# First unit's adaLN sums in two groups of two, with a new table of issue, in a two-layer trunk on one core

## The chip, the cores and the metric

One core of a Trainium2 chip runs the whole kernel. The metric is the device time of one execution in microseconds. The kernel before was timed three times: 294.76 us is the median (294.72 to 295.25).

## What is computed

The reference is a decoder trunk of two layers on one sequence of 256 tokens with 1024 features, all in float32. Each layer takes its shift, scale and gate from a conditioning vector `c` (adaLN), normalises, mixes and adds:

```python
for layer in range(DEPTH):                                   # DEPTH = 2
    ada = jnp.einsum('bd,de->be', c_act, w_ada[layer]) + b_ada[layer]
    shift, scale, gate = jnp.split(ada, 3, axis=-1)          # 1024 each
    h = rms_norm(x, norm_g[layer]) * (1.0 + scale[:, None, :]) + shift[:, None, :]
    y = even_mixer(h, ...) if layer % 2 == 0 else odd_mixer(h, ...)
    x = x + gate[:, None, :] * y
return rms_norm(x, final_g)
```

The even mixer projects `h` once (w_in_even), runs two groups of attention heads on the result, multiplies by gate paths and projects out. The odd mixer does the same with one group of 16 heads. The change concerns the product `c_act` times the shift and scale columns of `w_ada[0]`, which must be known before the first projection can use `h`.

## The kernel before, in words

The five engines are the tensor engine (PE), the vector engine (DVE), the scalar engine (ACT), GpSimd (POOL) and SyncE (SP); most transfers are started from SP's queue, and a few, `crow` (the vector c) and the first rows of biases among them, from ACT's. The projections run as three matmuls in a reduced float32 form, on a high and a low part of each operand (`whi`, `wlo`, `hhi`, `hlo`, made by ACT's casts and DVE's subtractions). The small sums of adaLN and the transposes run in full float32.

**The order of the work.** The program is first recorded: each call on an engine goes through `Plan.record`, gets the next number and a list of the records that it depends on. Then `Plan.issue` goes through the table `ORDER` of 3002 numbers and issues the records in that order. Each engine works strictly through its own part of that list, so the table decides what stands ahead of what on every engine and queue. `plan.group` ties records together only in their dependencies: every member of a group then waits for what any member waits for. As nearly all instructions are issued by one line of `Plan.issue`, the profile gives L244 for nearly all; tiles are what tells them apart.

**The start.** The input `x` comes into `xs`. ACT and DVE normalise it into the tiles `t` (one per half of the tokens), PE transposes these by a product with `ta` (an identity) in 16 pieces of 128x128 into the banks `ps_s` and `ps_pj`, and DVE and ACT copy them to `bigA`. PE also transposes `crow`; from it ACT and DVE make `cz`, where the activated c stands in column 0 of 32 with zeros beside it. Between these stand 26 dummy matmuls (`WARM`, `ps_o<-ones`), whose result is never used.

**The units.** The first projection consumes `h` in units of 2, 2, 2 and 2 tiles of 128 features (`START`). For each unit the loop at the end of the start loads the shift and scale columns of `w_ada[0]` and the rows of the projection's weights, calls `start_sums` to get this unit's shift and scale, `start_prep` to make `hhi` and `hlo`, and `start_mm` for the matmuls into the seven accumulating banks. `start_sums` has n = 2 tiles and d of the eight terms of each sum made by DVE beforehand (d = 0, 4, 4, 6). It has four sums to make, q = 0 and 1 the shift of the two tiles, q = 2 and 3 their scale. Each is a chain of matmuls with `cz[:, k]` as the stationary operand, 32 output rows and 128 columns, at rows 32q of one bank (`tile_position=(0, 32q)`), so that four of them with different q can use four quarters of the array. They are recorded with k outside and q inside, and tied together in fours. The first unit (d = 0) thus has 32 such matmuls: the tile `qT0` holds the shift columns for k = 0 to 3, `qT1` those for k = 4 to 7, `qT2` the scale columns for k = 0 to 3, and `gate` (in two loads) those for k = 4 to 7. Behind the sums, ACT copies the bank to `asb`, PE transposes it (`ps_m<-ta,asb`), DVE adds the bias and multiplies by the norm's weight, and `start_prep` can run. The second unit's weights are in `late`, the third's in `qT` and `gate` again, the fourth's in `late` again; in those units a DVE sum `acc` stands as one more term.

**The end.** The last projection ends in pieces. For the last 256 columns of the second half of the tokens, DVE adds PE's last bank to `xs` and forms the last sum of squares (`ISA parts`, in the profile CUSTOM_DVE_ANT_0 and its accumulator's read), POOL takes the root, and the output block is scaled (384 and 256 columns) and stored by SP and ACT. The 640 columns of the first half's output block, `t41` from `xs` and `parts`, are scaled by one instruction of DVE and stored by SP.

Of the kernel before, what the change touches and what calls it, by code (L numbers as in the profile page):

```python
# [255 lines left out]
def tile_trunk(  # L256
# [23 lines left out]
    plan = Plan(tc.nc)  # L280
# [433 lines left out]
    def start_sums(g, n, d, w):  # L714
# [29 lines left out]
        for o in range(0, len(ids), 4):  # L744
            plan.group(ids[o : o + 4])
# [640 lines left out]
```

## Time and profile before

| what | value |
|---|---|
| three runs | 294.76 us median, 294.72 to 295.25 |
| the profiled execution's own time | 295.04 us |
| its span, first to last instruction | 293.3 us |
| mean granted clock of PE | 0.995 |
| PE busy | 285.4 us (97%), 2293 instructions |
| DVE busy | 252.8 us (86%) |
| ACT busy | 188.5 us (64%) |
| DMA | 71.72 MB, mean 245 GB/s |
| chain that ended last | PE 82%, DMA 11% |

The profiled execution lies 0.28 us above the median, and 1.7 us of it lie outside the span. Times in the rows are microseconds from the start of the span; durations of single matmuls overlap, since they are pipelined, so the time that one takes is read from its start to the next one's start. A full-float32 matmul passes twice and leaves two records; in a row that joins several, the count is of records.

### The profile page before, as it was taken

What the parts mean: (1) busy time and instruction counts of PE and PEld (TensorE: products, weight loads), DVE (VectorE), ACT (ScalarE), POOL (GpSimd) and SP (SyncE); (2) the same over time, 40 slices, a digit from 0 to 9 for tenths busy, and PEclk for the clock granted to TensorE, in tenths of its full rate; (3) what the DMA queues carried; (4) which work ended last, traced back from release to release, by engine and by line L of the source; (5) the groups of instructions that cost most, each with busy time, mean ns of one, the idle gap of its engine ahead of it and who ended that gap; (6) DMA issues with size and microseconds to landing.
All of it is one profiled execution on the core that took longest, in us unless ns stands there. A gap on an engine that the chain in (4) does not pass through costs nothing.

```text
span 293.3 us, 6197 instructions
## 1 busy us (share of the span) xinstructions
PE 285.4 (97%) x2293; PEld 246.6 (84%) x2293; DVE 252.8 (86%) x629; ACT 188.5 (64%) x480; POOL 8.1 (3%) x33
## 2 busy tenths in 40 slices
PE   8999999999999999999999999999999999999991
PEld 8888788897897888777767899998899999887891
DVE  0497797999999999999889759779978999899884
ACT  4456256895998899994457863366658368584531
POOL 3000000000000000000020000000000000000021
PEclk9999999999999999999999999999999999999998
DMA  7999999999969942769986954569489709502003
GB/s 262 381 365 380 384 380 349 344 349 322 389 233 359 351 147 74 249 234 332 333 256 206 349 167 135 191 242 283 146 258 291 244 0 335 205 36 72 1 3 142
DMA packets 48431, 71.72 MB, mean 245 GB/s; under 512 B 2490, under 2 KB 33938, under 8 KB 48402
## 3 DMA queue, kind: packets, MB, share of 16 engines
q1 hardware_dynamic: 47906, 70.93, 70.6%
q8 instruction: 18, 0.29, 0.4%
q10 hardware_dynamic: 496, 0.41, 0.4%
q14 instruction: 11, 0.09, 0.1%
HBM read 70.28 MB, written 1.05 MB: 243 GB/s over the span
## 4 chain that ended last, share of the span: by engine, by line
PE 82%; DMA 11%; DVE 1%; ACT 1%; issue 1%; POOL 1%; POOLq 0%; DVEq 0%; ACTq 0%
PE ps_pj L244 53%; PE ps_s L244 10%; PE ps_o L244 7%; PE ps_pt L244 7%; PE ps_m L244 5%; DMA gate<-in_w_ada_dram 3%; DMA late<-in_w_ada_dram 3%; DMA raw<-in_w_in_even_dram 3%; DMA qT<-in_w_ada_dram 2%; DMA xs<-in_x_dram 1%; DVE wlo L244 1%; ACT t L244 1%; ACT whi L244 1%; POOL parts L244 1%; DVE t L244 0%
## 5 line engine op out<-in xcount | busy, mean ns | idle before, releaser
L244 ACT CAST whi<-raw 128x512 fp32r<-128x512 f32 (+2 forms) x116 | 71.8, 658 | 27.1 <-PE ps_pj L244 16.5
L244 DVE TENSOR_TENSOR wlo<-raw,whi 128x512 fp32r<-128x512 f32 (+2 forms) x100 | 71.3, 740 | 7.3 <-ACT whi L244 6.6
L244 PE MATMUL ps_pj<-hlo,whi 128*128 128x256 f32 x256 | 70.0, 288 | 0.0
L244 PE MATMUL ps_pj<-hhi,whi 128*128 128x256 f32 x256 | 69.9, 289 | 0.0
L244 PE MATMUL ps_pj<-hhi,wlo 128*128 128x256 f32 x256 | 68.3, 284 | 0.0
L244 PEld LDWEIGHTS ps_pj<-hhi,whi 128*128 128x128 f32 x256 | 46.7, 188 | 1.6 <-issue 0.7
L244 PEld LDWEIGHTS ps_pj<-hlo,whi 128*128 128x128 f32 x256 | 47.1, 189 | 0.8 <-issue 0.7
L244 PEld LDWEIGHTS ps_pj<-hhi,wlo 128*128 128x128 f32 x256 | 46.7, 189 | 0.3
L244 ACT ACTIVATE late<-late,mn 128x128 f32<-128x128 f32 (+1 forms) x58 | 26.0, 450 | 9.2 <-DVE mn L244 9.1
L244 DVE SCALAR_TENSOR_TENSOR acc<-raw,cz,acc 128x1024 f32<-128x1024 f32 x24 | 30.6, 1276 | 0.1
L244 PE MATMUL ps_pj<-whi,hlo 128*128 128x512 f32 (+2 forms) x72 | 25.6, 373 | 0.0
L244 PE MATMUL ps_pj<-wlo,hhi 128*128 128x512 f32 (+2 forms) x72 | 25.5, 372 | 0.0
L244 DVE SCALAR_TENSOR_TENSOR wlo<-raw,whi 128x512 fp32r<-128x512 f32 x32 | 21.1, 686 | 4.5 <-ACT whi L244 4.4
L244 PE MATMUL ps_pj<-whi,hhi 128*128 128x512 f32 (+2 forms) x72 | 24.8, 373 | 0.0
L244 PE MATMUL ps_pj<-wlo,ghi 128*128 128x512 f32 (+1 forms) x56 | 20.6, 371 | 0.0
L244 PE MATMUL ps_pj<-whi,ghi 128*128 128x512 f32 (+1 forms) x56 | 20.6, 371 | 0.0
L244 PE MATMUL ps_pj<-whi,glo 128*128 128x512 f32 (+1 forms) x56 | 20.4, 367 | 0.0
L244 PE MATMUL ps_pt<-ta,late 128*128 128x128 f32 x87 | 19.6, 275 | 0.0
L244 ACT COPY late<-ps_pt 128x384 f32<-128x384 f32 (+1 forms) x29 | 14.0, 483 | 7.9 <-PE ps_pt L244 7.6
L244 PEld LDWEIGHTS ps_pj<-whi,hhi 128*128 128x128 f32 x72 | 13.4, 188 | 2.5 <-ACT hhi L244 0.7
L244 PEld LDWEIGHTS ps_pj<-whi,hlo 128*128 128x128 f32 x72 | 13.6, 188 | 2.0 <-issue 0.2
L244 PEld LDWEIGHTS ps_pj<-wlo,hhi 128*128 128x128 f32 x72 | 13.4, 189 | 1.6
(243 smaller groups left out, 591.0 us busy)
## 6 DMA issues: line engine op xcount, KB each, us to landing
raw<-in_w_in_odd_dram SPq DMA_DIRECT2D x16, 1024.0 KB, 5.7
raw<-in_w_ada_dram SPq DMA_DIRECT2D x8, 1024.0 KB, 8.3
raw<-in_w_ada_dram SPq DMA_DIRECT2D x16, 512.0 KB, 6.3
raw<-in_w_in_even_dram SPq DMA_DIRECT2D x5, 1024.0 KB, 7.9
raw<-in_w_in_even_dram SPq DMA_DIRECT2D x7, 652.0 KB, 7.6
late<-in_w_ada_dram SPq DMA_DIRECT2D x16, 256.0 KB, 6.8
raw<-in_w_out_even_dram SPq DMA_DIRECT2D x4, 1024.0 KB, 5.8
raw<-in_w_out_odd_dram SPq DMA_DIRECT2D x4, 1024.0 KB, 8.7
```

The lines of the kernel that those rows point to most:

```text
L244: self.ops.append(dict(key=eng.key, deps=deps, fn=lambda: getattr(real, name)(*args, **kw)))
```

## The change

The records of `start_sums` are made in another order where d is 0, which is the first unit alone: first all eight steps of the two shift sums, then all eight of the two scale sums, tied together in twos. The other units keep the fours. The computed values are the same sums in the same order of k. The table `ORDER` is new from its first line on; two of its lines are shown, one taken out and one put in its place.

```diff
-5 0 45 4 9 685 2 3 6 10 37 7 1 85 11 40 38 35 86 12 87 13 14 15 16 17 70 18 88 19 89 20 71 21 72 22 55 23 46 41 39 42 47
+5 0 37 4 45 9 6 41 8 3 10 2 7 43 35 39 42 88 11 1 87 12 85 13 14 15 16 70 17 18 86 71 89 48 72 19 90 49 55 20 685 50 73
...
         ids = []
-        for m in range(max(len(tq) for tq in terms)):
-            for q, tq in enumerate(terms):
-                if m < len(tq):
+        size = 4 if d else 2
+        for o in range(0, 4, size):
+            for m in range(max(len(tq) for tq in terms)):
+                for q in range(o, o + size):
+                    tq = terms[q]
+                    if m >= len(tq):
+                        continue
                     ids.append(T.matmul(
                         pa[32 * q : 32 * q + 32, :P],
...
                         tile_position=(0, 32 * q),
                     ))
-        for o in range(0, len(ids), 4):
-            plan.group(ids[o : o + 4])
+        for o in range(0, len(ids), size):
+            plan.group(ids[o : o + size])
```

What the new table does is seen in the engines' lists. The first place is PE's list around the first unit's sums. Numbers behind an underscore are those of buffers, `x2` is a count of equal instructions in a row, and L244 of before is L245 of the change, whose table is one line longer. Before, the sums stand in one piece, shift and scale by turns:

```order
L244 MATMUL ps_s1_93<-ta_63,t41_89 128x128 x3
L244 MATMUL ps_m0_107<-qT0_98,cz_72 32x128 x2
L244 MATMUL ps_m0_107<-qT2_100,cz_72 32x128 x2
...
L244 MATMUL ps_m0_107<-qT1_99,cz_72 32x128 x2
L244 MATMUL ps_m0_107<-gate_77,cz_72 32x128 x2
L244 MATMUL ps_s1_93<-ta_63,t41_89 128x128
L244 MATMUL ps_pj1_95<-ta_63,t43_91 128x128
L244 MATMUL ps_m0_107<-ta_63,asb0_108 128x128
L244 MATMUL ps_pj1_95<-ta_63,t43_91 128x128
L244 MATMUL ps_o0_68<-ones_67 128x128
L244 MATMUL ps_pj1_95<-ta_63,t43_91 128x128
L244 MATMUL ps_o0_68<-ones_67 128x128 x3
L244 MATMUL ps_s1_93<-whi0_110,hhi_82 128x512
```

In the change the same place of PE's list reads:

```order
L245 MATMUL ps_m0_107<-qT2_100,cz_72 32x128 x8
L245 MATMUL ps_m0_107<-gate_77,cz_72 32x128 x2
L245 MATMUL ps_m0_107<-qT0_98,cz_72 32x128 x8
L245 MATMUL ps_m0_107<-gate_77,cz_72 32x128 x2
L245 MATMUL ps_s0_92<-ta_63,t41_89 128x128 x2
L245 MATMUL ps_m0_107<-qT1_99,cz_72 32x128 x8
L245 MATMUL ps_m0_107<-gate_77,cz_72 32x128 x4
L245 MATMUL ps_o0_68<-ones_67 128x128 x2
L245 MATMUL ps_m0_107<-ta_63,asb0_108 128x128
L245 MATMUL ps_o0_68<-ones_67 128x128 x5
L245 MATMUL ps_s0_92<-whi0_110,hhi_82 128x512
```

The sums now go by tiles: four pairs of scale, one more, four pairs of shift, one of scale, two transposes, then the rest of both. Four transposes of `t`, which stood behind the sums, have moved ahead of or between them, and seven dummies stand behind them where four stood. Ahead of the sums, PE has 22 dummies and 12 transposes of `t` before (15 dummies ahead of the transpose of `crow`), and 19 dummies and 14 transposes in the change (10 dummies ahead of that transpose).

The second place is the second unit's sums on PE, with the weights in `late`. Before they stand in one piece among the first unit's projection:

```order
L244 MATMUL ps_pj1_95<-wlo2_116,hhi_82 128x512
L244 MATMUL ps_s1_93<-whi2_112,hlo_83 128x512
L244 MATMUL ps_m0_107<-late_81,cz_72 32x128 x12
L244 MATMUL ps_m0_107<-acc0_106,ones_67 32x128 x4
L244 MATMUL ps_m0_107<-late_81,cz_72 32x128 x4
L244 MATMUL ps_pt0_85<-wlo3_117,hhi_82 128x256
```

In the change the first four of them come early in PE's list, six projection matmuls behind the first one:

```order
L245 MATMUL ps_pj1_95<-whi0_110,hhi_82 128x512
L245 MATMUL ps_pj2_96<-whi0_110,hhi_82 128x512
L245 MATMUL ps_m0_107<-late_81,cz_72 32x128 x4
L245 MATMUL ps_pt0_85<-whi1_111,hhi_82 128x256 x2
L245 MATMUL ps_pj2_96<-wlo0_114,hhi_82 128x512
```

The other sixteen follow some thirty rows later in one piece. On SP's queue, the loads of the first unit's adaLN weights go `gate`, `qT2`, `qT0`, `qT1`, `gate` where they went `qT0`, `qT1`, `qT2`, `gate`, `gate`, and the small loads of biases for later stages (`rows`, `srow`) come earlier. On ACT's queue the first rows of biases are started behind the table load, and no longer ahead of it.

The third place is the end of DVE's list. Before, the scaling of the 640 columns stands ahead of the last additions:

```order
L244 TENSOR_TENSOR xs_61<-xs_61,bigA_84 128x512
L244 TENSOR_SCALAR t41_89<-xs_61,parts_75 128x640
L244 TENSOR_TENSOR xs_61<-xs_61,bigA_84 128x256
L244 TENSOR_TENSOR xs_61<-xs_61,bigA_84 128x512
L244 TENSOR_TENSOR xs_61<-xs_61,ps_pj1_95 128x256
L244 ISA t42_90,parts_75<-xs_61,parts_75 128x256
L244 ISA parts_75 128x1
L244 TENSOR_SCALAR t40_88<-xs_61,parts_75 128x384
L244 SCALAR_TENSOR_TENSOR t40_88<-xs_61,parts_75,bigA_84 128x256
```

In the change it stands behind the last sum of squares:

```order
L245 TENSOR_TENSOR xs_61<-xs_61,bigA_84 128x512
L245 TENSOR_TENSOR xs_61<-xs_61,bigA_84 128x256
L245 TENSOR_TENSOR xs_61<-xs_61,ps_pj1_95 128x256
L245 ISA t42_90,parts_75<-xs_61,parts_75 128x256
L245 ISA parts_75 128x1
L245 TENSOR_SCALAR t41_89<-xs_61,parts_75 128x640
L245 TENSOR_SCALAR t40_88<-xs_61,parts_75 128x384
L245 SCALAR_TENSOR_TENSOR t40_88<-xs_61,parts_75,bigA_84 128x256
```

The scaling has moved past five instructions, the last addition of PE's result among them. PE's last 70 rows are the same in both.

231 rows, old and new, of the table ORDER are left out of this document.

## The prediction

> **What bounds the kernel now.** I read the busy time by stage first, then the chain of work that ended last, then the timeline of the tensor engine (PE) at the places that the change moves. By stage (columns: stretch and its length, then busy time of each engine with its number of instructions, granted clock, DMA share, GB/s):
>
> ```profile
> core 0: us, PE busy (x) PEld busy (x) DVE busy (x) ACT busy (x) POOL busy (x), PEclk, DMA share, GB/s
> 7.00:14.70 7.70, 7.66 (x110) 6.67 (x108) 3.65 (x13) 3.09 (x8) 0.71 (x3) 1.00 1.08 384
> 14.70:32.00 17.30, 17.30 (x125) 14.68 (x124) 14.91 (x31) 9.28 (x21) 0.00 (x0) 1.00 1.07 372
> 32.00:45.00 13.00, 12.50 (x118) 10.27 (x118) 11.08 (x23) 5.45 (x12) 0.00 (x0) 1.00 1.06 384
> 45.00:274.00 229.00, 229.00 (x1841) 197.69 (x1842) 210.08 (x535) 160.96 (x421) 2.48 (x7) 1.00 0.70 238
> ```
>
> PE fills every stretch except for 0.5 us between 32 and 45. Its last matmul starts at 286.78:
>
> ```profile
> 286.78 0.27 PE L244 MATMUL ps_pj<-whi,glo 128*128 128x256 f32 x1
> ```
>
> So from 7 to 287 us the program lasts as long as PE's list of work. The chain puts DMA ahead of PE only near the start; its row for the second half of the tile `gate`, the last adaLN weight of the first unit, gives issue and time to landing:
>
> ```profile
> 4.16 7.62 DMA gate<-in_w_ada_dram
> ```
>
> It has landed at 4.16 + 7.62 = 11.78. PE's timeline up to the first projection (start, duration, operation, out<-in, records; a full-float32 matmul leaves two records, a transpose one):
>
> ```profile
> 7.67 1.38 PE L244 MATMUL ps_o<-ones 128*128 128x128 f32 x10
> 8.88 0.27 PE L244 MATMUL ps_pj<-ta,t 128*128 128x128 f32 x1
> 8.99 0.39 PE L244 MATMUL ps_o<-ones 128*128 128x128 f32 x2
> ...
> 11.05 1.18 PE L244 MATMUL ps_m<-qT,cz 128*32 128x128 f32 x34
> ...
> 12.06 0.28 PE L244 MATMUL ps_m<-qT,cz 128*32 128x128 f32 x2
> 12.07 0.28 PE L244 MATMUL ps_m<-gate,cz 128*32 128x128 f32 x2
> ...
> 12.73 0.28 PE L244 MATMUL ps_m<-gate,cz 128*32 128x128 f32 x2
> 12.94 0.33 PE L244 MATMUL ps_s<-ta,t 128*128 128x128 f32 x1
> 13.10 0.27 PE L244 MATMUL ps_pj<-ta,t 128*128 128x128 f32 x1
> ...
> 14.74 0.70 PE L244 MATMUL ps_s<-whi,hhi 128*128 128x512 f32 x2
> ```
>
> The first sums run from 11.05 to 12.94, and the landing at 11.78 was past when PE came to the last fours. So PE's own list, and not the landing, decides that the first projection starts at 14.74. What the change adds to that list ends up in the time, unless it falls into the one wait at 32.
>
> **The sums in pairs.** The 32 matmuls of the first unit stay. A matmul with 32 output rows takes a quarter of the array, and four of them with different quarters run together. The third unit's sums give the price of a four, and hold the wait:
>
> ```profile
> 31.82 0.58 PE L244 MATMUL ps_pj<-whi,hhi 128*128 128x408 f32 x2
> 32.89 0.64 PE L244 MATMUL ps_m<-qT,cz 128*32 128x128 f32 x16 [0.50 <-DMA qT<-in_w_ada_dram]
> ...
> 33.57 0.40 PE L244 MATMUL ps_m<-acc,ones 128*32 128x128 f32 x8
> 33.79 0.40 PE L244 MATMUL ps_m<-gate,cz 128*32 128x128 f32 x8
> ```
>
> From 33.57 to 33.79 one four (8 records) takes 0.22 us, and eight fours 8 x 0.22 = 1.76. No pair of 32-row matmuls stands in this trace. The nearest rows are the pairs of 64-row matmuls of the attention values:
>
> ```profile
> 91.20 1.52 PE L244 MATMUL ps_o<-late,vb 128*64 128x256 f32 x16
> 92.65 0.49 PE L244 MATMUL ps_s<-late,qT 64*128 64x128 f32 x4
> ```
>
> These 16 records are four pairs, two of 256 and two of 128 columns; 2 x 0.44 + 2 x 0.22 = 1.32, and 1.45 was taken with the change of shape behind them. So a pair costs what a four costs. The first unit then has 16 steps in the place of 8, or +1.76, if no pair overlaps another. But at three seams of the new order a scale pair stands next to a shift pair, which write other quarters, and the rows at 12.06 and 12.07 show matmuls from two buffers begin 0.01 apart when their quarters differ. Then it is 13 steps, +5 x 0.22 = +1.10. I take 1.10, for that row shows the mechanism, and keep 1.76 as the upper end. The Trainium skill, TensorEngine Tiling (Array Packing), section Key Properties, says that different tiles can load weights and multiply in parallel. By that rule the sum is the 1.10 too, by a strict reading of the groups 1.76; the fours of this trace agree with the rule, and no run here has a seam.
>
> **Changes of shape.** The new order puts two transposes between the first unit's sums, and sends the second unit's first four ahead alone. Each is one more trip of PE into 32-row shape and back. Its price, from the second unit's sums:
>
> ```profile
> 21.51 0.39 PE L244 MATMUL ps_pj<-wlo,hhi 128*128 128x512 f32 x1
> 21.74 0.40 PE L244 MATMUL ps_s<-whi,hlo 128*128 128x512 f32 x1
> 22.07 0.86 PE L244 MATMUL ps_m<-late,cz 128*32 128x128 f32 x24
> ...
> 23.08 0.43 PE L244 MATMUL ps_m<-late,cz 128*32 128x128 f32 x8
> 23.43 0.39 PE L244 MATMUL ps_pt<-wlo,hhi 128*128 128x256 f32 x1
> 23.66 0.35 PE L244 MATMUL ps_o<-whi,hlo 128*128 128x408 f32 x1
> ```
>
> The 512-column matmul at 21.74 takes 0.33 to its successor where the one at 21.51 took 0.23 (+0.10); the last four 0.35 where 0.22 is usual (+0.13); the 256-column one at 23.43 takes 0.23, twice its usual half of a 512 (+0.11). That is 0.34 a trip. Around transposes it is 0.21 - 0.11 = 0.10 in front of 12.94 and 0.16 - 0.11 = 0.05 behind it, and with 0.10 going in again about 0.27.
>
> **The start, added up.** Of 26 dummies, 4 stood behind the sums, of 16 transposes of x 4 (the `asb` one apart); now 7 and none, with two transposes among the sums. So ahead of the sums stand 3 dummies fewer (2 records of 0.11 each) and 2 transposes more (0.11, from 8.88 to 8.99): -0.66 + 0.22 = -0.44. Then +1.10, two transposes +0.22 and their trip +0.27: the sums end 1.15 later. From the last sum to the first projection it was 14.74 - 12.73 = 2.0, a chain of copy, transpose, scale and shift on three engines, which stays; the seven dummies in it (7 x 0.22 = 1.54) fit. I take off 0.1 for the first transposes: at 7.67 ten dummy records last to 8.88, 1.21 where 1.11 would do, since PE waited there for the scalar engine's half, which the new order has earlier. So the first projection at 14.74 + 1.05 = 15.8. The vector and scalar engines lose nothing: weights and their casts get a microsecond more of lead.
>
> From there on: +0.34 for the second unit's trip. Against it stands the wait: from 31.82 two 408-column matmuls take 0.37 and the change of shape 0.10, so PE was ready at 32.29 and began at 32.89. At 1.4 us later it is ready at 33.7, behind that landing, and 0.60 of the delay is gone; what is late next is the fourth unit's landing, below. PE's balance is +1.05 + 0.34 - 0.60 = +0.8.
>
> **The rest of the order.** From 45 to 274 the same matmuls of the same shapes stand in another order, and PE was full there (229.00 of 229.00). There is nothing to win but short waits inside that busy span, and nothing to lose but new ones: 0, with 0.3 either way as my choice. SP's small loads that move ahead (16 rows of 512 bytes) weigh nothing at 372 GB/s.
>
> **The end.** PE's last 70 rows are the same. Behind them the vector engine (DVE) changes:
>
> ```profile
> 285.84 0.55 DVE L244 TENSOR_SCALAR t<-xs,parts 128x640 f32<-128x640 f32 x1
> ...
> 287.25 0.41 DVE L244 TENSOR_TENSOR xs<-xs,ps_pj 128x256 f32<-128x256 f32 x1
> ...
> 288.22 0.08 DVE L244 DVE_READ_ACCUMULATOR2_ANT parts<- 128x1 f32 x1
> 288.96 0.42 DVE L244 TENSOR_SCALAR t<-xs,parts 128x384 f32<-128x384 f32 x1 [0.67 <-POOL parts L244]
> ```
>
> PE is done at 286.78 + 0.27 = 287.05, but DVE came only at 287.25, held by its queue. Now the scaling of the 640 columns (0.55) stands behind the last sum of squares, in the wait of 0.67 for POOL's root, and no longer ahead of it: DVE is free in time, -0.15. But that block's 320 KB go out later:
>
> ```profile
> 286.43 3.81 SPq L244 DMA_DIRECT2D out_dram<-t  x3
> 287.10:288.20 1.10, 0.00 (x0) 0.00 (x0) 0.95 (x3) 0.00 (x0) 0.00 (x0) 1.00 0.74 298
> 290.10:292.00 1.90, 0.00 (x0) 0.00 (x0) 0.00 (x0) 0.00 (x0) 0.00 (x0) 0.59 0.78 276
> ```
>
> They went in 1.1 us, some 0.7 after their issue at 286.43; the last four pieces (1.90 us at 276 GB/s) followed from 290.1. Now the block is issued near 288.7, moves from 289.4 to 290.5, and the last pieces, 0.15 earlier at 290.0, share half a microsecond with it: 0.5 - 0.15 = +0.35 at most, -0.15 if the sharing is free. I take +0.2.
>
> **The sum** against the profiled execution: 295.04 + 0.8 + 0.2 = 296.0. That run is 0.28 above the median of 294.76, so the median to expect is 294.76 + 1.0 = 295.8. A measurement here tells about 0.2%, 0.59 us, from no change.
>
> **Rivals.** *The front moves up by half a microsecond more (no change).* The transpose of `crow` now stands behind 10 dummies, not 15, and what waits for it can start up to two microseconds sooner. DVE was held by it:
>
> ```profile
> 7.98 0.16 DVE L244 SCALAR_TENSOR_TENSOR tiny<-tiny,ps_pt 128x8 f32<-128x8 f32 x1 [1.24 <-ACT tiny L244]
> ```
>
> If more of PE's time ahead of 11.05 was hand-over than the 0.1 that I see, the first projection comes at 15.3, and with the end at -0.15 it is +0.55 + 0.34 - 0.60 - 0.15 = +0.15: 294.9. For it: that row; against it: PE busy for 7.66 of 7.70. Chance 0.25.
>
> *The landing leads the start (faster).* The change sums the scale's first half before the last landing. If PE were through with all but the last two pairs at 11.78, the last sum would start near 12.2 in the place of 12.73, and the first projection at 14.2. The second trip takes 0.34 back; the third unit's sums stand some 0.5 us of work later than before, so that the wait at 32.89 goes as well: -0.5 + 0.34 - 0.5 = -0.66, 294.1 with the end unchanged. It decides itself at the first sum: it must start 2.4 us (11 of 13 steps) before 11.78, at 9.4, with 14 transposes and 19 dummies ahead. By the list it starts at 10.6. Chance 0.10.
>
> *No overlap at the seams (slower still).* +0.65, and part of the wait stays if the landing slips with the small loads: +1.6 to +2.2, about 296.7. Chance 0.12.
>
> That the order is undone can be left out: the built program has the pairs.
>
> **The numbers.** The forecast, +0.6 to +1.6, has the remaining 0.53. Slower 0.53 + 0.12 = 0.65, same 0.25, faster 0.10. The range leaves out about 2 in 10: down to the first rival's +0.15 less the 0.3 of the order's middle, -0.15, 294.6; up to 1.05 + 0.65 + 0.34 - 0.30 (half the wait) + 0.3 + 0.2 = +2.24, 297.0.
>
> **What would show it.** Right: the first 32-row sum at 10.1 to 10.6 and the last about 3.4 later; the first projection near 15.8; no idle time ahead of the third unit's sums; the fourth unit's, now beginning here, about 0.8 later:
>
> ```profile
> 44.08 0.43 PE L244 MATMUL ps_m<-late,cz 128*32 128x128 f32 x8
> ```
>
> PE's last matmul near 287.6; the 640-column output moving with the last ones. Wrong: a first projection before 15.0, a pair in 0.11, or PE idle by over 0.3 us anywhere between 45 and 274.

## The result, and the profile after

The changed kernel took 296.26 us (median of five runs, 295.84 to 297.0) beside 294.76 for the kernel before (294.72 to 295.28): 1.0051 of it, 95% interval 1.0038 to 1.0063. On a second chip, twelve runs of it beside 23 of the kernel before gave 1.0031 (1.002 to 1.0041). By the medians it is slower by 1.0 to 1.5 us; the forecast was +1.0 and 295.8. The profiled execution took 296.94, with a span of 295.0 where before had 293.3.

The busy time by stage of the changed kernel, in the same stretches as before:

```profile
core 0: us, PE busy (x) PEld busy (x) DVE busy (x) ACT busy (x) POOL busy (x), PEclk, DMA share, GB/s
7.00:14.70 7.70, 7.05 (x98) 6.17 (x97) 2.54 (x8) 2.48 (x7) 0.64 (x3) 1.00 1.08 373
14.70:32.00 17.30, 17.30 (x129) 14.48 (x128) 14.07 (x32) 9.85 (x22) 0.00 (x0) 1.00 1.07 371
32.00:45.00 13.00, 13.00 (x102) 10.71 (x100) 11.26 (x24) 5.11 (x11) 0.00 (x0) 1.00 1.05 376
45.00:274.00 229.00, 228.79 (x1860) 198.27 (x1860) 209.29 (x536) 161.59 (x421) 3.04 (x9) 1.00 0.71 240
```

The wait of 0.5 us between 32 and 45 is gone, as forecast. Two new ones have come: 0.65 ahead of 14.7 and 0.21 behind 45. PE's timeline at the start shows the first:

```profile
7.96 0.21 PE L245 MATMUL ps_pt<-ta,rows 24*128 24x24 f32 x1 [0.65 <-DMA rows<-in_b_ada_dram]
...
10.89 1.10 PE L245 MATMUL ps_m<-qT,cz 128*32 128x128 f32 x20
...
12.58 0.44 PE L245 MATMUL ps_s<-ta,t 128*128 128x128 f32 x2
12.95 0.96 PE L245 MATMUL ps_m<-qT,cz 128*32 128x128 f32 x14
13.66 0.30 PE L245 MATMUL ps_m<-gate,cz 128*32 128x128 f32 x2
...
13.80 0.50 PE L245 MATMUL ps_m<-gate,cz 128*32 128x128 f32 x6
14.22 0.71 PE L245 MATMUL ps_o<-ones 128*128 128x128 f32 x4
...
16.04 0.71 PE L245 MATMUL ps_s<-whi,hhi 128*128 128x512 f32 x2
```

The transpose of the biases' rows stands early in the new list, and in this execution their transfer had not landed. The sums last from 10.89 to 14.22, 3.33 where they took 1.89, and the first projection starts at 16.04, 1.30 later than before. Some 0.24 of the 3.33 is a second landing: the last load of `gate`, issued at 4.48, landed 9.1 later, at 13.6, and the pairs that need it begin at 13.66, 0.71 behind the row at 12.95. In the second profile of the same program (after_2, below) that load landed at 11.9, those pairs begin 0.47 behind that row, and the sums last 3.09. The third and the fourth unit's sums and PE's last matmul:

```profile
34.44 0.65 PE L245 MATMUL ps_m<-qT,cz 128*32 128x128 f32 x16
...
45.25 0.43 PE L245 MATMUL ps_m<-late,cz 128*32 128x128 f32 x8
...
288.24 0.28 PE L245 MATMUL ps_pj<-whi,glo 128*128 128x256 f32 x1
```

No wait stands at the third unit. PE ends 1.46 later than before. Behind 45 the order of 229 us of work is new, and one wait in it is new. Before, the transposes of `t` follow the projection at once (0.23 from start to start):

```profile
150.33 0.39 PE L244 MATMUL ps_s<-whi,glo 128*128 128x512 f32 x1
150.56 0.66 PE L244 MATMUL ps_pj<-ta,t 128*128 128x128 f32 x4
```

After, PE waits there for DVE, and 0.61 passes in place of 0.23, which is +0.38 (0.21 of it is marked as idle, since the row ahead lasts 0.40):

```profile
151.65 0.40 PE L245 MATMUL ps_s<-whi,glo 128*128 128x512 f32 x1
152.26 0.55 PE L245 MATMUL ps_pj<-ta,t 128*128 128x128 f32 x3 [0.21 <-DVE t L245]
```

DVE is late there because the root that POOL takes ahead of it is longer. Before, it has no instruction of DVE beside it:

```profile
149.43 0.55 POOL L244 TENSOR_TENSOR parts<-parts,expo 128x1 f32<-128x1 f32 x1 [0.93 <-DVE shs L244]
```

After, DVE's list has a weight's subtraction there, and the root takes 0.93, which is 0.38 more:

```profile
150.59 0.69 DVE L245 TENSOR_TENSOR wlo<-raw,whi 128x512 fp32r<-128x512 f32 x1
150.75 0.93 POOL L245 TENSOR_TENSOR parts<-parts,expo 128x1 f32<-128x1 f32 x1 [2.43 <-DVE parts L245]
```

This root takes 0.55 in the profiles of the old table and 0.93 or 0.94 in those of the new one. No run puts this one subtraction back, so the link to the wait is read from the rows and not tested alone.

The end of the program after (DVE, POOL, SP):

```profile
288.55 0.42 DVE L245 TENSOR_TENSOR xs<-xs,ps_pj 128x256 f32<-128x256 f32 x1 [0.34 <-PE ps_pj L245]
...
289.53 0.55 DVE L245 TENSOR_SCALAR t<-xs,parts 128x640 f32<-128x640 f32 x1
290.52 0.42 DVE L245 TENSOR_SCALAR t<-xs,parts 128x384 f32<-128x384 f32 x1 [0.44 <-POOL parts L245]
...
289.69 0.79 POOL L245 TENSOR_TENSOR parts<-parts,expo 128x1 f32<-128x1 f32 x1 [0.93 <-DVE parts L245]
...
290.10 1.70 SPq L245 DMA_DIRECT2D out_dram<-t  x3
```

DVE now takes PE's last bank 0.03 after its end (288.52) and no longer 0.20 after it: -0.17. But POOL's root takes 0.79, and its row before says 0.55:

```profile
288.38 0.55 POOL L244 TENSOR_TENSOR parts<-parts,expo 128x1 f32<-128x1 f32 x1 [1.93 <-DVE parts L244]
```

So the last scaling starts 0.99 behind the end of DVE's squares (289.53 to 290.52) and not 0.74 (288.22 to 288.96), +0.25. From PE's last start to the end of the span it is 6.76 in place of 6.52. In the profile, +1.46 for PE and +0.24 for the end make the +1.70 of the span. The execution's own time is 1.90 longer (296.94 against 295.04); the other 0.2 lies outside the span, and no row tells what it is.

### The profile page after: what moved, and what is told of

It is laid out like the page before. It is cut to its first block, busy times and chain, and to the rows that moved or that the text cites. A ratio compares the mean times of both kernels' runs of the same rounds, so it can differ in the third digit from the quotient of the medians.

```text
span 295.0 us, 6190 instructions
## 1 busy us (share of the span) xinstructions
PE 286.5 (97%) x2293; PEld 247.9 (84%) x2293; DVE 251.8 (85%) x629; ACT 189.3 (64%) x480; POOL 8.9 (3%) x33
## 3 DMA queue, kind: packets, MB, share of 16 engines
HBM read 70.28 MB, written 1.05 MB: 242 GB/s over the span
## 4 chain that ended last, share of the span: by engine, by line
PE 93%; DMA 2%; DVE 1%; issue 1%; POOL 1%; ACT 0%; POOLq 0%; ACTq 0%; DVEq 0%
PE ps_pj L245 59%; PE ps_s L245 11%; PE ps_o L245 9%; PE ps_pt L245 8%; PE ps_m L245 7%; DMA rows<-in_b_ada_dram 2%; DVE t L245 1%; POOL parts L245 1%; DVE xs L245 0%; POOLq L1386 0%; ACTq L245 0%; ACT t L245 0%; DVEq L1386 0%; ACT L245 0%; DVE shs L245 0%
## 5 line engine op out<-in xcount | busy, mean ns | idle before, releaser
L245 ACT CAST whi<-raw 128x512 fp32r<-128x512 f32 (+2 forms) x116 | 72.1, 656 | 21.6 <-PE ps_pj L245 12.1
L245 DVE TENSOR_TENSOR wlo<-raw,whi 128x512 fp32r<-128x512 f32 (+2 forms) x100 | 71.6, 741 | 5.4 <-ACT whi L245 5.1
L245 PE MATMUL ps_pj<-hhi,wlo 128*128 128x256 f32 x256 | 70.0, 291 | 0.0
L245 PE MATMUL ps_pj<-hhi,whi 128*128 128x256 f32 x256 | 70.0, 289 | 0.0
L245 PE MATMUL ps_pj<-hlo,whi 128*128 128x256 f32 x256 | 68.3, 285 | 0.0
L245 PEld LDWEIGHTS ps_pj<-hhi,whi 128*128 128x128 f32 x256 | 47.2, 189 | 1.8 <-issue 0.7
L245 PEld LDWEIGHTS ps_pj<-hhi,wlo 128*128 128x128 f32 x256 | 46.8, 189 | 0.2
L245 PEld LDWEIGHTS ps_pj<-hlo,whi 128*128 128x128 f32 x256 | 46.5, 189 | 0.4
L245 ACT ACTIVATE late<-late,mn 128x128 f32<-128x128 f32 (+1 forms) x58 | 26.0, 449 | 10.4 <-DVE mn L245 10.3
L245 DVE SCALAR_TENSOR_TENSOR acc<-raw,cz,acc 128x1024 f32<-128x1024 f32 x24 | 30.7, 1278 | 0.0
L245 PE MATMUL ps_pj<-whi,hhi 128*128 128x512 f32 (+2 forms) x72 | 25.5, 376 | 0.0
L245 PE MATMUL ps_pj<-wlo,hhi 128*128 128x512 f32 (+2 forms) x72 | 25.5, 373 | 0.0
L245 PE MATMUL ps_pj<-whi,hlo 128*128 128x512 f32 (+2 forms) x72 | 25.4, 373 | 0.0
L245 DVE SCALAR_TENSOR_TENSOR wlo<-raw,whi 128x512 fp32r<-128x512 f32 x32 | 21.4, 684 | 3.9 <-ACT whi L245 3.9
L245 PE MATMUL ps_pj<-wlo,ghi 128*128 128x512 f32 (+1 forms) x56 | 20.7, 370 | 0.0
L245 PE MATMUL ps_pj<-whi,ghi 128*128 128x512 f32 (+1 forms) x56 | 20.5, 369 | 0.0
L245 PE MATMUL ps_pj<-whi,glo 128*128 128x512 f32 (+1 forms) x56 | 20.3, 369 | 0.0
L245 PE MATMUL ps_pt<-ta,late 128*128 128x128 f32 x87 | 20.0, 277 | 0.0
L245 ACT COPY late<-ps_pt 128x384 f32<-128x384 f32 (+1 forms) x29 | 14.0, 484 | 8.7 <-PE ps_pt L245 8.6
L245 PEld LDWEIGHTS ps_pj<-whi,hhi 128*128 128x128 f32 x72 | 13.4, 188 | 2.4 <-ACT hhi L245 0.6
L245 PEld LDWEIGHTS ps_pj<-whi,hlo 128*128 128x128 f32 x72 | 13.4, 189 | 1.9 <-issue 0.2
L245 PEld LDWEIGHTS ps_pj<-wlo,hhi 128*128 128x128 f32 x72 | 13.5, 190 | 1.5 <-DVE wlo L245 0.2
```

What stands on the lines that cost most here:

```text
L245: self.ops.append(dict(key=eng.key, deps=deps, fn=lambda: getattr(real, name)(*args, **kw)))
```

## The experiments

Two theories. **Theory 1**: the steps of the first unit's sums, and PE's list at the start, carry the difference. **Theory 2**: the start moves from run to run with the landings, the old table absorbs such moves in its waits and the new one does not, and the table behind the start costs as much as the start. Landmarks of all profiles, from their timelines (start of the first projection, of the third unit's sums, of PE's last matmul; us), and the ratio to the kernel before on the same chip. By the records, 1128 more columns of projection stand ahead of the third unit's sums in the new table, about 0.5 us of work (512 columns take 0.23), so distances to that landmark are compared only within one table. The last distance counts from the start of PE's last matmul; the expectations below count from its end, 0.27 later.

| run | first proj. | third unit | PE's last | first proj. to PE's last | PE's last to end | ratio (95%) |
|---|---|---|---|---|---|---|
| before | 14.74 | 32.89 | 286.78 | 272.04 | 6.52 | |
| before_2 | 14.32 | 32.96 | 286.85 | 272.53 | 6.55 | 1.0009 (0.9997 to 1.0021) |
| b_fewer | 14.58 | 32.57 | 286.49 | 271.91 | 6.61 | 1.0010 (0.9995 to 1.0026) |
| b_pairs | 15.63 | 33.05 | 287.04 | 271.41 | 6.56 | 1.0016 (1.0 to 1.0031) |
| b_tail | 14.30 | 32.80 | 286.73 | 272.43 | 6.87 | 1.0016 (1.0002 to 1.003) |
| h_start | 15.00 | 34.08 | 287.89 | 272.89 | 6.61 | 1.0041 (1.0028 to 1.0054) |
| after | 16.04 | 34.44 | 288.24 | 272.20 | 6.76 | 1.0051 (1.0038 to 1.0063) |
| after_2 | 14.89 | 33.27 | 287.11 | 272.22 | 6.79 | 1.0031 (1.002 to 1.0041) |
| h_rest | 14.25 | 40.09 | 293.86 | 279.61 | 6.84 | 1.0234 (1.0217 to 1.0251) |
| a_u1 | 15.04 | 33.25 | 287.03 | 271.99 | 6.87 | 1.0034 (1.0022 to 1.0046) |
| a_tail | 14.96 | 33.54 | 287.40 | 272.44 | 6.60 | 1.0014 (1.0004 to 1.0025) |
| a_fours | 15.51 | 33.93 | 287.75 | 272.24 | 6.85 | 1.0050 (1.0038 to 1.0062) |
| a_fours_loads | 14.99 | 33.71 | 287.83 | 272.84 | 6.87 | 1.0050 (1.0038 to 1.0062) |
| a_loads | 16.73 | 35.13 | 288.92 | 272.19 | 6.78 | 1.0060 (1.0043 to 1.0076) |

**a_fours: the changed kernel with fours.** The 32 places of the table are filled in the order of the fours.

```diff
-        size = 4 if d else 2
+        size = 4
```

> The changed kernel with the first unit's 32 sums again in fours (eight steps), in the same places of the new table; loads as in the change (gate, qT2, qT0, qT1, gate). Theory 1 (PE's list sets the start): 13 steps become 8, 5 x 0.22 = 1.1 us less, so the first projection moves from 16.04 to about 14.95 and the time from 296.3 to about 295.2. Rival (the landing sets it): in the change the last adaLN weights landed at 13.62 in place of 11.78, so PE must stand in front of the last two fours; they end at 13.62 + 0.44 + 0.1 = 14.16 where the pairs ended at 14.22, the first projection stays at 16.0, PE is idle by about 1 us ahead of the last fours, and the time stays at 296.2.

Measured: 296.46 us, 1.0050. The 1.1 us did not come back. PE stands twice in front of a landing:

```profile
10.68 1.08 PE L245 MATMUL ps_m<-qT,cz 128*32 128x128 f32 x32 [0.39 <-DMA qT<-in_w_ada_dram]
12.18 0.30 PE L245 MATMUL ps_m<-qT,cz 128*32 128x128 f32 x2 [0.42 <-DMA qT<-in_w_ada_dram]
...
15.51 0.71 PE L245 MATMUL ps_s<-whi,hhi 128*128 128x512 f32 x2
```

With scale loaded ahead of shift, a four must wait for the later of two tiles, which is what the pairs avoid. Theory 1 as I put it falls here. The rival's numbers did not come either (a first projection at 16.0, a wait ahead of the last two fours): in this execution the two waits stand ahead of the first and the fifth four, and the projection starts at 15.51.

**a_fours_loads and a_loads: the first unit's loads in the old order**, once with fours, once with pairs. SP's list:

```diff
-gate qT2 qT0 qT1 gate
+qT0 qT1 qT2 gate gate
```

> The same with the first unit's loads back in the old order (qT0, qT1, qT2, gate, gate); everything else of the new table stays. Theory 1: as the run with fours alone, about 295.2, since only the steps count. Rival: only here the 1.1 us appears, because both the steps and the landing are those of before; 295.1 against 296.2 with the new loads. If the last landing stays at 13.6 with the old order of loads, the order of loads is not what moved it, and this run reads like the one with fours alone.

> The changed kernel, pairs kept, with only the first unit's five loads back in the old order. Theory 1: PE's list is the same, so nothing changes: 296.3 within 0.3, first sum at 10.9, first projection at 16.0. Rival: the slow transfers between 4.5 and 7 us (180 to 300 GB/s in place of 290 to 400) come from the new order of loads; with the old one the biases' rows land before PE asks for them (0.65 us of idle time at 7.96 goes), and the time is about 295.7.

Measured: 296.51 and 296.74. With fours and old loads the first projection comes at 14.99, yet PE's last matmul stands where it stood with the new loads (287.83 and 287.75): the distance between grew from 272.24 to 272.84. What the start gained was lost on the way, some 0.3 of it ahead of the third unit's sums and the rest behind them, with no single wait that the profile marks. With pairs and old loads PE waits longer, since the pairs ask for the scale first and it lands last:

```profile
7.87 0.21 PE L245 MATMUL ps_pt<-ta,rows 24*128 24x24 f32 x1 [1.12 <-DMA rows<-in_b_ada_dram]
...
11.75 1.17 PE L245 MATMUL ps_m<-qT,cz 128*32 128x128 f32 x19 [0.89 <-DMA qT<-in_w_ada_dram]
```

The rows of the biases are late here too, so they can be late without the new order of loads; that part of the rival falls.

**b_pairs: the kernel before with pairs**, its own table, the sums in one piece.

```diff
+        size = 4 if d else 2
+        for o in range(0, 4, size):
...
-            plan.group(ids[o : o + 4])
+            plan.group(ids[o : o + size])
```

> The kernel before with its own table, and only the first unit's 32 sums made in pairs, in the order that the change has for them but in one piece without transposes between: 13 steps if a scale pair and a shift pair overlap where they meet, 16 if not. Theory 1: sums from 11.05 last 1.1 us longer (1.76 without overlap), the first projection at 15.85 (16.5), 0.6 of it goes into the wait ahead of the third unit's sums at 32.89: 294.76 + 0.5 = 295.3 (295.9 without overlap). Rival: the later start is given back elsewhere and the time stays at 294.8, or the pairs cost half a four and it stays at 294.8 too; then the first projection stands at 14.8.

Measured: 295.33 beside 295.06, 1.0016. PE's timeline:

```profile
11.22 1.10 PE L245 MATMUL ps_m<-qT,cz 128*32 128x128 f32 x20 [0.80 <-DMA qT<-in_w_ada_dram]
12.09 0.31 PE L245 MATMUL ps_m<-gate,cz 128*32 128x128 f32 x2
12.16 0.28 PE L245 MATMUL ps_m<-qT,cz 128*32 128x128 f32 x2
...
13.61 0.28 PE L245 MATMUL ps_m<-gate,cz 128*32 128x128 f32 x2
...
15.63 0.71 PE L245 MATMUL ps_s<-whi,hhi 128*128 128x512 f32 x2
...
33.05 0.42 PE L245 MATMUL ps_m<-qT,cz 128*32 128x128 f32 x8
```

From the first record of the sums to the last it is 2.40 (11.22 to 13.62) where fours took 1.68 (1.80 in before_2): pairs cost 0.72 at most and not 1.10. The first row says why. Four scale pairs stand first, which is 16 records; the row counts 20 up to 12.09. The other four belong to shift pairs, and these stand in PE's list behind the `gate` pair that starts at 12.09. The changed kernel's own row at 10.89 counts 20 in the same place. So shift runs ahead of scale by more than the one step at a seam: 0.72 / 0.22 is 3.3 steps, not 5. By the single records the first shift pair starts with the fourth scale pair (11.88 and 11.92) and not with the fifth, and the 16 pairs stand in 11 steps, not 13. And the first projection is 0.89 later than in the profile of before, PE's last matmul only 0.26: the rest went into the wait at the third unit. Of the 0.89, 0.17 is a sum that started later, behind the landing in the first row.

**after_2: the changed kernel again.**

> The changed kernel as it is, beside its variants on one chip and for a second profile. Both theories: 1.003 to 1.006 of the kernel before. Theory 1 (PE's list at the start): first projection again at 16.0. Theory 2 (the table behind the start, and landings that move from run to run): the first projection shifts by up to 0.7 from one profile to the next, with the landing of the biases' rows (7.8 in the first profile), while the time from the first projection to PE's last matmul is again 272.2.

Measured: 295.94 beside 294.96, 1.0031. The second profile:

```profile
6.41 0.21 PE L245 MATMUL ps_pt<-ta,rows 24*128 24x24 f32 x1
...
9.99 1.10 PE L245 MATMUL ps_m<-qT,cz 128*32 128x128 f32 x20
...
13.08 0.71 PE L245 MATMUL ps_o<-ones 128*128 128x128 f32 x4
...
14.89 0.71 PE L245 MATMUL ps_s<-whi,hhi 128*128 128x512 f32 x2
...
287.11 0.27 PE L245 MATMUL ps_pj<-whi,glo 128*128 128x256 f32 x1
```

The rows had landed, and the same program starts its projection 1.15 earlier: 0.90 at the first sum, and 0.24 by the last load of `gate`, which had landed too. From there to PE's last matmul it is 272.22, and 272.20 in the first profile: the whole difference goes through to the end, as theory 2 has it.

**h_rest and h_start: halves of the two tables.** All engines' lists up to the first projection from the one, the rest from the other.

```diff
-start of the change, rest of the change
+h_rest:  start of before, rest of the change
+h_start: start of the change, rest of before
```

> The start of the kernel before (all engines up to the first projection: loads, dummies, transposes, sums in fours), and the table of the change from there on. Theory 1: only the second unit's extra trip (0.34, into a wait of 0.6) and the end (0.2) are left: 294.8 + 0.2 = 295.0, no change. Theory 2: the rest carries most of it: trip 0.34, the middle 0.24, the end 0.3, and waits for landings up to 57 us take what the earlier start gives: 1.003 to 1.005, 295.7 to 296.3, with the first projection at 14.8.

> The start of the change (loads, dummies, transposes, sums in pairs) and the table of the kernel before from the first projection on. Theory 1: nearly all of the change is here: first projection at 16.0, 1.3 later, less the wait of 0.6 at 32.89: 1.0025, 295.5. Theory 2: the later start finds its landings made and costs less: 0.2 to 0.5, 1.001 to 1.002, and the sum of this run's and the other half's excess is more than the change's.

Neither half can be read as meant, because the loads of the units behind the start are cut with the start. h_rest took 302.21 us, 1.0234 (1.0217 to 1.0251): the second unit's early four asks for a tile that the old order of loads brings late.

```profile
21.01 0.66 PE L245 MATMUL ps_m<-late,cz 128*32 128x128 f32 x8 [4.60 <-DMA late<-in_w_ada_dram]
```

h_start took 296.46, with a new wait for a weight's low part, which DVE there makes only at 22.57, behind its `acc` sums:

```profile
23.31 0.50 PE L245 MATMUL ps_pj<-wlo,hhi 128*128 128x512 f32 x1 [1.16 <-DVE wlo L245]
```

They show that the lists of PE, DVE and SP are fitted to each other, and leave the shares of the halves open.

**a_u1: the second unit's sums in one piece again.**

```diff
-L245 MATMUL ps_m0_107<-late_81,cz_72 32x128 x4
...
-L245 MATMUL ps_m0_107<-late_81,cz_72 32x128 x8
+L245 MATMUL ps_m0_107<-late_81,cz_72 32x128 x12
```

> The changed kernel with only the second unit's first four sums moved back to stand with its other sixteen. If the extra trip into 32-row shape costs PE 0.34 (theory 1 and 2 alike) and nothing takes it back, the distance from the first projection to PE's last matmul falls from 272.2 to 271.9 and the time by 0.3, 1.002 where the second runs of the change had 1.003. Rival: the later sums make the second unit's shift and scale late, or a landing takes the 0.34: distance 272.2, same time.

Measured: 296.02, 1.0034. The distance falls from 272.21 to 271.99: the trip costs PE 0.22 where I had 0.34. In the time it is lost within the intervals (1.0034 here, 1.0031 for the change on another chip).

**a_tail and b_tail: the end alone**, undone in the change and made in the kernel before (lists of DVE, ACT, POOL, SP). 21 places of DVE's list differ, 7 of ACT's and 2 of POOL's; the last part of DVE's, as b_tail has it:

```diff
-L245 TENSOR_SCALAR t41_89<-xs_61,parts_75 128x640
 L245 TENSOR_TENSOR xs_61<-xs_61,bigA_84 128x256
 L245 TENSOR_TENSOR xs_61<-xs_61,bigA_84 128x512
 L245 TENSOR_TENSOR xs_61<-xs_61,ps_pj1_95 128x256
 L245 ISA t42_90,parts_75<-xs_61,parts_75 128x256
 L245 ISA parts_75 128x1
+L245 TENSOR_SCALAR t41_89<-xs_61,parts_75 128x640
```

> The changed kernel with only the end of the lists of DVE, ACT, POOL and SP (behind the last-but-one pieces of the output projection) in the order of before: the first half's root and its two output pieces come some 3 us earlier. From PE's last matmul to the end of the span it is 6.23 before and 6.46 in the change. If the end costs what it seems to, this run gets 0.2 to 0.35 back: 1.004 where the change has 1.005; if the output's pieces do not matter, the distance stays at 6.46 and the time the same.

> The kernel before with only the end of the lists of DVE, ACT, POOL and SP in the order of the change. If the order of the end costs by itself, the distance from PE's last matmul to the end of the span goes from 6.25 to 6.5 and the time up by 0.25 to 0.4, 1.001; POOL's last root takes 0.79 in place of 0.55 because DVE's scaling of 640 columns runs beside it. As forecast ahead of the result (DVE 0.15 earlier, shared output 0.35 at most) it would be +0.2.

Measured: a_tail 295.53, 1.0014 where the change had 1.0031 on the same chip; b_tail 295.35, 1.0016 where the kernel before had 1.0009 (before_2). From PE's last matmul to the end 6.60 and 6.87. The two intervals of each pair overlap, so the times alone don't settle it, but the profiles say the same of the end from both sides. The runs move the end as a whole; that the root is what costs is read from the rows. b_tail (DVE, POOL):

```profile
288.02 0.55 DVE L245 TENSOR_SCALAR t<-xs,parts 128x640 f32<-128x640 f32 x1
289.01 0.42 DVE L245 TENSOR_SCALAR t<-xs,parts 128x384 f32<-128x384 f32 x1 [0.44 <-POOL parts L245]
...
288.18 0.79 POOL L245 TENSOR_TENSOR parts<-parts,expo 128x1 f32<-128x1 f32 x1 [0.93 <-DVE parts L245]
```

And POOL's root in a_tail, with no scaling beside it:

```profile
289.00 0.55 POOL L245 TENSOR_TENSOR parts<-parts,expo 128x1 f32<-128x1 f32 x1 [1.93 <-DVE parts L245]
```

**b_fewer: the kernel before without five dummies.**

```diff
-WARM = 26
+WARM = 21
```

> The kernel before without five of its 26 dummy matmuls, those that stand last ahead of the transpose of crow (left out: work whose result is never used). Theory 1 (PE's list bounds the start): the sums start 1.1 us earlier, 9.9 in place of 11.05, the last fours wait for the landing at 11.8, the first projection comes at 14.1 and the time falls by 0.6 to 294.1, 0.998. Theory 2 (what the start gains is taken at the next landings): first projection at 14.1 as well, but the wait ahead of the third unit's sums grows from 0.6 to 1.2 and the time stays within 0.2.

Measured: 294.93 beside 295.0, 1.0010 (0.9995 to 1.0026). The start does not take what the shorter list offers. PE now waits for x's tiles and for a weight's landing:

```profile
7.51 0.33 PE L245 MATMUL ps_pj<-ta,t 128*128 128x128 f32 x1 [0.69 <-ACT t L245]
...
10.77 0.43 PE L245 MATMUL ps_m<-qT,cz 128*32 128x128 f32 x8 [0.20 <-DMA qT<-in_w_ada_dram]
...
14.58 0.71 PE L245 MATMUL ps_s<-whi,hhi 128*128 128x512 f32 x2
```

So PE's list alone did not bound the old start; by this profile it stood about even with the data. It is one execution, and a late landing in it is not excluded. The wait at the third unit did not grow to 1.2 either, so theory 2's number for it falls with the earlier start that it needed.

**before_2: the kernel before again.**

> The kernel before once more, for a second profile and as a measure of the comparison itself: 1.000. Theory 2: its first projection moves between profiles as that of the change does (14.9 and 16.0), by several tenths of a us, and the wait ahead of the third unit's sums moves against it, so that PE's last matmul stays within 0.3 of 286.8. Theory 1: first projection at 14.7 within 0.1 again.

Measured: 1.0009, which is how far the comparison of a kernel with itself strays. Its profile:

```profile
14.32 0.47 PE L244 MATMUL ps_s<-whi,hhi 128*128 128x512 f32 x1
...
19.53 0.39 PE L244 MATMUL ps_pt<-whi,hhi 128*128 128x256 f32 x1 [0.31 <-ACT whi L244]
...
32.96 0.64 PE L244 MATMUL ps_m<-qT,cz 128*32 128x128 f32 x16 [0.32 <-DMA qT<-in_w_ada_dram]
```

With the old table the first projection lies between 14.30 and 15.63 in five profiles (h_start, with its new wait, left aside), the third unit's sums between 32.57 and 33.05: of 1.33 that the start moves, 0.48 are left. The wait at the third unit takes part of it, and in before_2 and b_tail a wait for ACT's `whi` near 19.5 takes 0.31 and 0.36. With the new table four of the profiles (after, after_2, a_fours, a_loads) have 18.38 to 18.42 between the two landmarks, over starts from 14.89 to 16.73. Two others lost more, without a marked wait: a_tail (14.96) has 18.58 and a_fours_loads (14.99) has 18.72. No version tried beats the kernel before.

Neither theory stands whole. Of theory 1, the pairs cost 0.72 in the profile of b_pairs, but taking them out of the change (a_fours) gave no time back, since landings held the fours. Of theory 2, the new table lets most moves of the start through, but not that of a_fours_loads. Behind the start it takes 0.80 more than the old table does without waits (272.21 against 271.41 in b_pairs).

## Why the prediction was right, point by point

**Sign and size.** Mean of the two profiles of each kernel: the first projection at 15.47 against 14.53, +0.94 (forecast +1.05); from there to PE's last matmul 272.21 against 272.29, -0.08 (forecast +0.34 - 0.60 + 0 = -0.26); the end 6.78 against 6.54, +0.24 (forecast +0.2). The sum is +1.10 against +1.0, and the two chips measured +1.5 and +1.0. The sign was reasoned, but that the sum comes so near is in part luck: the pairs were put 0.4 too high and the trip 0.12 too high, and the middle, put at 0, cost 0.58 (below). The start's +0.94 is the mean of +1.30, with two late landings, and +0.57 in the second profiles, without them. Two of the prediction's own signs of being wrong came: a first projection before 15.0 (14.89 in after_2), and, counted from start to start, 0.38 lost at one place between 45 and 274 (152.26).

**The pairs.** "So a pair costs what a four costs" held. "Then it is 13 steps, +5 x 0.22 = +1.10" was mis-sized: 0.72 in b_pairs. I had counted an overlap of one step at each seam; shift pairs went further ahead, and scale pairs too, for 11 steps in all. The rival without overlap falls.

**The sums' start.** This step failed in the profiled execution: I had the first sum at 10.1 to 10.6 and it came at 10.89; in the second profile it came at 9.99, 0.57 ahead of before_2's 10.56, where the list alone gave 0.44 and the first transposes 0.1. I read the start from one execution of before, as PE's list alone, and did not ask when the rows' transfer lands that the new list asks for earlier. b_fewer shows the same from the other side: with 1.1 us of list taken out ahead of the sums, the first projection came at 14.58, no earlier than before_2's 14.32.

**The trips.** The two transposes with their trip were costed at 0.22 + 0.27 = 0.49. From 12.58 to 12.95 it is 0.37, and the last matmuls ahead of them take 0.21 to the next start where 0.11 is usual: 0.47, as costed. The second unit's trip measured 0.22 (a_u1), not 0.34.

**The wait at the third unit** went, as forecast, and that is what let the start through to the end. "What is late next is the fourth unit's landing" did not come: its sums stand at 45.25 without a wait, 1.17 later than before and not 0.8, and in after_2 at 44.08, where they stood before.

**The middle.** "0, with 0.3 either way" was too narrow below by what it hid: one new wait, +0.38 at 152.26. With the old table and no wait at the third unit (b_pairs) it is 271.41 from the first projection to PE's last matmul, and 272.21 in the change: 0.80, of which 0.22 are the trip and 0.38 that wait. The other 0.2 I could not assign. What the forecast left out here is what it left out at the end (next point): the new order of DVE's list puts an instruction beside a root of POOL's, which takes 0.93 and not 0.55.

**The end.** +0.24 by the profile where I had +0.2, but by other parts. DVE's -0.15 came (-0.17). The shared output cost little at most: the last issue on ACT's queue is 1.55 later than before (291.00 against 289.45) and the span's end 1.70, which leaves 0.15 for it. What I had not seen is POOL's root, +0.25. The Trainium skill, GPSIMD Engine Reference, section Specifications, says that GpSimd's way into the on-chip memory is shared with VectorE and contended for by some of its instructions. The rows agree: 0.55 without DVE's scaling beside it and 0.79 with it, in each table both ways; whether the scaling is one of those instructions no row shows. The root's length goes by the DVE instruction that runs when it begins: it ends 0.40 behind the end of the scaling (290.08 to 290.48) and 0.41 behind that of the subtraction at 150.59 (151.28 to 151.69). In all 14 profiles every root of 0.66 or more began during an instruction of DVE and ended 0.40 to 0.42 behind it. Not every instruction does this: a root begun during a scaling of DVE's from PE's bank (155.04 in the changed kernel) took 0.55.

The first rival (the front moves up, no change) had its mechanism: against before_2 the second profile's first projection is 0.57 later, where the rival had +0.55. But the time was still 1.0031, since the wait at the third unit was gone and the end cost its 0.24. The faster rival needed a first sum at 9.4, and 9.99 was the earliest seen.

## What to carry to other kernels

A start read from one execution is one draw: ask of each step that moves forward in a list when its data lands, and take two profiles before a difference of half a microsecond is believed. A wait in the middle of a tuned order is also a cushion: with the old table 1.3 us of movement at the start left 0.5 at the third unit, and with the new one, in four profiles, all of it reached the end. Where an engine's list is reordered, look at what runs beside the last short steps on the other engines; a root of 0.55 us became 0.79 because a scaling was put beside it, and another became 0.93 beside a subtraction, and both times the engine behind the root lost about as much.

## What was not expected of the hardware

Each engine was said above to work strictly through its part of the list. For matmuls on different quarters of the array these traces show otherwise: shift pairs began ahead of a `gate` pair that stands before them (20 records up to 12.09 in b_pairs where 16 were due, and up to 11.79 in the changed kernel), and pairs in an order of 13 steps took 0.72 more than fours and not 1.10. The same program's first projection moved by 1.15 us between two executions (16.04 and 14.89), and POOL's root took 0.55 us alone, 0.79 beside DVE's scaling of 640 columns and 0.93 beside a subtraction of 512, ending 0.40 to 0.41 behind either.
